# Two-layer decoder trunk on one core: the row sums of layer A's first products move from VectorE to GpSimd and are used one block later

## The chip, the core and the metric

The kernel runs on one core of a Trainium2 chip. The engines are TensorE (PE in the profile, its weight loads PEld), VectorE (DVE), ScalarE (ACT), GpSimd (POOL) and SyncE (SP), which issues the DMA transfers. The metric is the device time of the program in microseconds, as a median over runs; lower is better. A difference is told in microseconds and as a share of the time before.

## The reference, cut to what matters

The program is a two-layer decoder on a sequence of 2048 positions and a width of 1024, in float32. Layer A takes an RMS norm, makes one combined projection into query, key, value, forget logits and gate, attends with a decaying bias, and projects back; layer B shares keys and values and attends in a window of 128. Only the head of layer A is touched by the change:

```python
def rmsnorm(x, g):
    xf = x.astype(jnp.float32)
    y = xf * lax.rsqrt(jnp.mean(xf * xf, axis=-1, keepdims=True) + EPS)
    return (y * g.astype(jnp.float32)).astype(x.dtype)
...
u = rmsnorm(h, norm_a_g[i])
proj = u @ w_in_a[i]
q, k, v, f_logit, gate = jnp.split(
    proj, [WIDTH_A, 2 * WIDTH_A, 3 * WIDTH_A, 3 * WIDTH_A + N_HEADS_A], axis=-1)
```

The gain `g` is folded into the weights, and the factor `rsqrt(mean(x*x) + EPS)` of a row is multiplied in only when the product leaves PSUM.

## The kernel before, in words

The sequence is cut into 16 blocks of 128 positions (`tb`). Layer A's projection runs over seven groups of columns; a group's weights are eight pairs of tiles (`wh` and `wl`, high and low part of 128 rows of the weight matrix, `dt` 0 to 7), and for each block three matmuls per `dt` (high times high, high times low, low times high) add up in one PSUM bank of tag `b2`, of which there are three. Group 0 makes the first half of the values. It is special, since the input arrives during it.

For each block x comes transposed from HBM into a tile `xt` of tag `st` (even blocks, and all from block 12 on) or `wr` (odd blocks). `split_block` makes the high part `uh` on ScalarE (L385) and the low part `ul` on VectorE (L386). Then `block_squares` squares `xt` in place on ScalarE (L391) and adds its eight pieces of 128 columns on VectorE in one TENSOR_REDUCE (L393) into a tile of tag `ro2`, of which there are two. `block_sums` multiplies the two sums of a pair of blocks by a column of ones on TensorE (L402), so that a sum over all 1024 features lies in PSUM; `rstd` (L359 to L365, with one square root on ScalarE, L360) turns it into the factors of both blocks. `v_tile` then takes a block's bank out: a high part on ScalarE (L541) and a low part on VectorE (L542), into a tile of tag `st` (four of them), which one DMA writes to HBM (L545).

`factor(tb, dt)` says when: at an even `tb`, the squares of this block and the next are asked for at `dt` 0, the sums and factors at `dt` 7. `v_tile` of a block follows its last matmul. `constants` makes, among others, `fold` and `identb` from a unit matrix on VectorE (L229 to L234); both are first read in layer A's attention. `vectors`, called at block 8, loads small vectors.

The program text is not the order of execution. A scheduler orders the instructions of each engine when the kernel is built, by what it expects them to cost, within what the tiles allow; each engine then runs its own list strictly in order, and waits on semaphores for others. So what is written later may run earlier, and an instruction that waits holds up all that stand behind it in its engine's list.

Of the kernel before, what the change touches and what calls it, by code (L numbers as in the profile page):

```python
# [18 lines left out]
ALU = mybir.AluOpType  # L19
AX = mybir.AxisListType  # L20
# [3 lines left out]
P = 128  # L24
S = 2048
D = 1024
NTB = S // P
NDT = D // P
# [4 lines left out]
CH = 512  # L33
# [24 lines left out]
NORM_AHEAD = 2  # L58

LOADED_AHEAD = 3  # L60
QK_LAG = 1

FACTOR_AT = 7
ROW_AT = 2

JOBS_AT = (0, 3, 6, 9)
# [85 lines left out]
class Trunk:  # L152
# [56 lines left out]
    def constants(self):  # L209
        nc, cp, a = self.nc, self.const, self.a  # L210

        def select(view, src, pattern, base, cm, fill):
            nc.gpsimd.affine_select(
                out=view, in_=src, pattern=pattern, compare_op=ALU.is_ge,
                fill=fill, base=base, channel_multiplier=cm,
            )

        def tile_(name, shape, dt=F32):
            return cp.tile(shape, dt, name=name, tag=name)

        self.ones = tile_("ones", [P, P])
        nc.gpsimd.memset(self.ones, 1.0)
        self.tri = tile_("tri", [P, P])
        select(self.tri, self.ones, [[1, P]], 0, -1, 0.0)
        self.ident = tile_("ident", [P, P])
        select(self.ident, self.tri, [[-1, P]], 0, 1, 0.0)

        self.fold = tile_("fold", [P, 32])
        nc.vector.tensor_tensor(self.fold, self.ident[:, :32], self.ident[:, 32:64], ALU.add)  # L229
        for c in (64, 96):  # L230
            nc.vector.tensor_tensor(self.fold, self.fold, self.ident[:, c : c + 32], ALU.add)
        nc.vector.tensor_single_scalar(self.fold, self.fold, 2.0, ALU.mult)
        self.identb = tile_("identb", [P, P], BF16)
        nc.vector.tensor_copy(self.identb, self.ident)  # L234

        self.mask_s = tile_("mask_s", [P, 2, P], BF16)
        nc.gpsimd.memset(self.mask_s, 0.0)
        for i in range(2):
            select(self.mask_s[:, i], self.mask_s[:, i], [[1, P]], 0, -1, NEG)

        self.band = tile_("band", [P, 2, P], BF16)
        nc.gpsimd.memset(self.band[:, 0], 0.0)
        select(self.band[:, 0, :], self.band[:, 0, :], [[-1, P]], 0, 1, NEG)
        nc.vector.tensor_tensor(self.band[:, 1], self.tri, self.ident, ALU.subtract)

        self.loads = []
# [24 lines left out]
        self.g_kv = column("g_kv", a["kv_norm_g"], NDT)  # L271
        self.g_qb = pair_column("g_qb", a["qnorm_b_g"][0])
        self.g_kb = pair_column("g_kb", a["knorm_b_g"])
        self.sink = row("sink", a["sinks"], H)
        self.gq16 = row("gq16", a["qnorm_b_g"][:, :ROT], ROT)
# [6 lines left out]

    def vectors(self):

        nc = self.nc
        self.load_vectors(self.loads[1:])
        for t in (self.g_qb, self.g_kb):
            for s in range(2):
                nc.vector.memset(t[s * HD : s * HD + ROT, :], 1.0)

        nc.vector.tensor_single_scalar(self.g_qb, self.g_qb, HD**-0.5, ALU.mult)
# [96 lines left out]
    def block_squares(self, xt):  # L388

        nc = self.nc  # L390
        nc.scalar.activation(xt, xt, AF.Square)  # L391
        sums = self.sb("ro2", [P, P])
        nc.vector.tensor_reduce(sums, xt.rearrange("p (c t) -> p t c", t=P), AX.X, ALU.add)  # L393
        return sums

    def block_sums(self, both, tb):
# [169 lines left out]
    def normer(self, src):  # L566
# [41 lines left out]

        def factor(tb, dt):

            both = (tb, tb + 1)
            if tb % 2:
                return
            if turned and dt == 0:
                for b in both:
                    blocks[b] = self.block_squares(blocks[b])
            if dt == FACTOR_AT:
                sm = self.sb("sm", [P, 4, 8], bufs=4) if turned else small[tb]
                ss = self.block_sums([blocks[b] for b in both], tb) if turned else None
                self.rstd(sm, 2, D, ss=ss, out=factors[:, tb : tb + 2])  # L620

        return upto, factor, uh, ul, factors, fetch

    def projections(self, normed, groups, row, later=None, pre=None, hook=None, first=None):
# [75 lines left out]
        for gi, grp in enumerate(groups):  # L700
# [35 lines left out]
                continue  # L736
            q, v = grp.get("qk"), grp.get("v")
            rope = self.rotary(q["rope"]) if q and "rope" in q else None
            late = []
            for tb in range(NTB):  # L740
                norm(tb + NORM_AHEAD)
                if gi == 1 and tb == ROW_AT:
                    self.rstd_row(factors, row)
                r0 = factors[:, tb : tb + 1]
                if gi == 0 and pre is not None and tb in pre:
                    pre[tb]()
                if tb in FORGET_AT and forget:
                    forget.pop(0)()
                if gi and tb in JOBS_AT and jobs:
                    jobs.pop(0)()  # L750
                us = slice(tb % 4 * P, (tb % 4 + 1) * P)
                ps = self.ps("b2", [P, CH])
                for dt in range(NDT):
                    if hook is not None and gi == len(groups) - 1:
                        hook(tb, dt)
                    if gi == 0:
                        factor(tb, dt)
                    for i, (u, k) in enumerate(((uh, 0), (uh, 1), (ul, 0))):
                        nc.tensor.matmul(  # L759
                            ps[:, :n], u[tb // 4][:, dt, us], W[k][dt],  # L760
                            start=(dt == 0 and i == 0), stop=(dt == NDT - 1 and i == 2),
                        )
                if len(late) > QK_LAG:
                    late.pop(0)()
                if q is not None:
                    c0 = q["c0"]
                    qn = self.qk_norm(
# [9 lines left out]
                if v is not None:  # L777
# [4 lines left out]
                        ),  # L782
                        r0,
                    )
            for job in late:
                job()
            if grp.get("forget"):
# [835 lines left out]
```

## Time and profile before

| What | Value |
|---|---|
| Time, median of 3 runs | 2460.58 us (2459.92 to 2462.29) |
| The profiled execution: its time, its span | 2461.66 us, 2459.7 us |
| PE busy | 2424.1 us, 99% of the span |
| PEld, DVE, ACT, POOL busy | 82%, 70%, 51%, 41% of the span |
| Group 0 of layer A | about 8 to 105 us of the span |

The profile's views that are used: the table of busy times by engine; busy times in stretches of the span; the list of who waited for whom; the timeline of one engine, with the idle time before an instruction and what ended it in brackets; groups of instructions by line and shape with the mean duration of one. The busy share of PE says that the program is bound by TensorE nearly everywhere, so that a change shows in the time only where TensorE waits.

### The profile page before, as it was taken

Reading aid. Unit: us, or ns where it says so; the run is one execution under the profiler, and the core shown is the slowest. Engines: PE = TensorE matmul, PEld = TensorE weight load, DVE = VectorE, ACT = ScalarE, POOL = GpSimd, SP = SyncE. Lnnn points to the kernel's source line nnn. Section 1 sums busy time; section 2 is a strip of 40 time slices with the busy share of each in tenths; the row PEclk is TensorE's granted clock in tenths of the full one; section 3 lists DMA queues with packets and bytes.
Section 4 is the critical chain, followed back from the end, with each engine's and each line's share of the span. In section 5 each row is a group of like instructions: output and inputs, shape, how many; then the busy total and the mean of one; then the engine's idle time right before and its main releaser. Section 6 shows DMA issues by size and latency. Waiting matters only on the chain.

```text
span 2459.7 us, 36240 instructions
## 1 busy us (share of the span) xinstructions
PE 2424.1 (99%) x12016; PEld 2022.4 (82%) x12016; DVE 1727.4 (70%) x3826; ACT 1255.1 (51%) x2504; POOL 1001.9 (41%) x643
## 2 busy tenths in 40 slices
PE   8999999999999999999999999999999999999999
PEld 6788899988888887878877778888788888888887
DVE  7656567735888888888888866456766523777776
ACT  5433324323777777777777761135323312555554
POOL 0000000012877777777778862210011000377775
PEclk9999999999999999999999999999999999999999
DMA  6656545687554655465456649975434415555552
GB/s 181 207 165 193 156 145 168 192 261 223 168 155 128 210 141 150 143 198 164 133 168 182 169 137 306 290 253 153 139 90 120 137 64 165 174 176 178 180 180 73
DMA packets 351515, 419.24 MB, mean 170 GB/s; under 512 B 64928, under 2 KB 248256, under 8 KB 345152
## 3 DMA queue, kind: packets, MB, share of 16 engines
q1 hardware_dynamic: 351328, 416.92, 56.6%
q8 instruction: 95, 1.56, 0.3%
q14 instruction: 92, 0.75, 0.1%
HBM read 265.29 MB, written 151.40 MB: 169 GB/s over the span
## 4 chain that ended last, share of the span: by engine, by line
PE 46%; DVE 4%; DMA 2%; ACT 2%; POOL 2%; issue 2%; SPq 0%; DVEq 0%; ACTq 0%; POOLq 0%
PE b L759 9%; PE b L1240 5%; PE pa L1027 5%; PE pb L1453 4%; PE pb L722 3%; PE pb L1066 3%; PE b L722 3%; PE mx L936 2%; PE sc L985 2%; PE sc L984 2%; PE pa L1383 1%; PE b L1304 1%; PE pa L722 1%; PE pa L1240 1%; PE pb L1240 1%
## 5 line engine op out<-in xcount | busy, mean ns | idle before, releaser
L759 PE MATMUL b<-wh,big 128*128 128x512 f32 (+3 forms) x2560 | 770.1, 375 | 9.8 <-ACT wh L486 8.7
L1003 POOL TENSOR_TENSOR big<-st,big 128x1024 fp32r<-128x1024 f32 (+1 forms) x320 | 657.9, 2070 | 261.4 <-ACT big L1002 155.6
L759 PEld LDWEIGHTS b<-wh,big 128*128 128x128 f32 x2560 | 471.3, 188 | 81.2 <-ACT wh L486 10.5
L759 PE MATMUL b<-wl,big 128*128 128x512 f32 (+3 forms) x1280 | 474.2, 371 | 1.9 <-DVE wl L487 1.9
L1012 DVE TENSOR_TENSOR ac<-ac,st 128x512 f32<-128x512 f32 (+3 forms) x576 | 355.4, 617 | 55.6 <-ACT st L999 27.2
L999 ACT ACTIVATE st<-sc 128x512 f32<-128x512 f32 (+1 forms) x512 | 274.3, 585 | 161.8 <-PE sc L985 79.0
L1027 PE MATMUL pa<-big 128*128 128x512 f32 (+3 forms) x1280 | 326.1, 369 | 3.9 <-POOL big L1003 1.8
L1002 ACT CAST big<-st 128x1024 fp32r<-128x1024 f32 (+1 forms) x320 | 295.6, 924 | 7.8
L759 PEld LDWEIGHTS b<-wl,big 128*128 128x128 f32 x1280 | 241.4, 189 | 38.3 <-DVE wl L487 6.1
L1027 PEld LDWEIGHTS pa<-big 128*128 128x128 f32 x1280 | 222.0, 189 | 50.3 <-ACT sq L1035 17.0
L947 DVE CUSTOM_DVE_ANT_0 mx<-mx,rot 128x128 f32<-128x128 f32 (+3 forms) x240 | 210.7, 878 | 40.9 <-PE mx L936 34.8
L495 ACT ACTIVATE sq<-b,r 128x512 f32<-128x512 f32 (+2 forms) x128 | 77.8, 608 | 301.6 <-PE b L759 298.6
L984 PE MATMUL sc<-big 128*128 128x512 f32 (+3 forms) x640 | 230.1, 364 | 1.3 <-DVE st L542 1.1
L985 PE MATMUL sc<-big 67*128 67x512 f32 (+3 forms) x640 | 229.0, 367 | 0.0
L936 PE MATMUL mx<-big 66*128 66x128 f32 (+3 forms) x660 | 191.1, 363 | 3.6 <-DVE mt L947 3.1
L1066 PE MATMUL pb<-wh,wr 128*128 128x512 f32 x488 | 179.3, 398 | 2.8 <-DMA wr<-wg 2.2
L859 POOL MEMSET rot<- 128x1024 bf16 x1 | 1.0, 952 | 420.8 <-PE pb L349 420.8
L497 DVE TENSOR_REDUCE sm<-sq 128x8 f32<-128x512 f32 (+2 forms) x128 | 74.9, 585 | 138.6 <-ACT sq L495 138.4
L1352 POOL TENSOR_TENSOR big<-big,tri 128x1024 fp32r<-128x1024 f32 x60 | 143.8, 2397 | 67.1 <-DVE big L1349 62.2
L936 PEld LDWEIGHTS mx<-big 66*128 66x128 f32 x660 | 114.1, 190 | 40.9 <-DVE mt L947 11.9
L984 PEld LDWEIGHTS sc<-big 128*128 128x128 f32 x640 | 121.0, 189 | 23.1 <-DVE st L542 1.5
L985 PEld LDWEIGHTS sc<-big 67*128 67x128 f32 x640 | 121.2, 189 | 21.0
(281 smaller groups left out, 4124.8 us busy)
## 6 DMA issues: line engine op xcount, KB each, us to landing
wr<-wg SPq DMA_DIRECT2D x62, 512.0 KB
va<-st SPq DMA_DIRECT2D x32, 512.0 KB
ka<-st SPq DMA_DIRECT2D x64, 256.0 KB
ut<-big SPq DMA_DIRECT2D x16, 1024.0 KB
big<-ka SPq DMA_DIRECT2D x16, 1024.0 KB
big<-qa SPq DMA_DIRECT2D x16, 1024.0 KB
qb<-st SPq DMA_DIRECT2D x64, 256.0 KB
big<-qb SPq DMA_DIRECT2D x16, 1024.0 KB
```

The costliest lines, as they stand in the source:

```text
L722: nc.tensor.matmul(ps, W[k][dt][:, ft * P : (ft + 1) * P], u[ch][:, dt, :], start=(dt == 0 and i == 0), stop=(dt == NDT - 1 and i == 2),)
L759: nc.tensor.matmul(ps[:, :n], u[tb // 4][:, dt, us], W[k][dt], start=(dt == 0 and i == 0), stop=(dt == NDT - 1 and i == 2),)
L936: mm = nc.tensor.matmul(ps[:, b, :wb], qb[:66, i * P : (i + 1) * P], kb[:66, k0 + b * wb : k0 + (b + 1) * wb], start=True, stop=True,)
L947: nc.vector.tensor_tensor_reduce(out=lg, in0=lg, in1=mask, scale=1.0, scalar=NEG, op0=ALU.add, op1=ALU.max, accum_out=f_(o),)
L984: nc.tensor.matmul(o, ka[:, ks], qa[:, qs], start=not (last and n_), stop=False)
L985: nc.tensor.matmul(o, kb[:, ks], qb[:, qs], start=False, stop=not diag)
L999: nc.scalar.activation(pf[:, off : off + w], ps[:, :w], AF.Exp, scale=HD**-0.5)
L1002: nc.scalar.copy(ph[:, :tw], pf[:, :tw])
L1003: nc.gpsimd.tensor_tensor(pl[:, :tw], pf[:, :tw], f_(ph[:, :tw]), ALU.subtract)
L1012: nc.vector.tensor_tensor(a_, a_, pf[:, off : off + w], ALU.add)
L1027: nc.tensor.matmul(pv[:, q0 : q0 + w], v[:, k, :], src[:, off : off + w], start=(p == 0 and n_ == 0 and i == 0), stop=(last and n_ == 1 an ...
L1066: nc.tensor.matmul(ps, w[:, dt // 2 % 2, wk, dt % 2, :], us[dt][uk], start=(dt == 0 and i == 0), stop=(dt == NDT - 1 and i == 2),)
```

## The change

Three things change. (1) The eight pieces of a block's squares are no longer added by one TENSOR_REDUCE on VectorE, but by three adds on GpSimd: 512 columns onto 512, 256 onto 256, and 128 plus 128 into the `ro2` tile. (2) The sums and factors of a pair are asked for at `dt` 3 of the odd block, not at `dt` 7 of the even one; the even block's `v_tile` is held back until then, and both blocks are taken out after it. (3) `fold` and `identb` are made in `vectors` instead of `constants`.

```diff
+TURNED_AT = 3
+
+SQUARES_AT = 6
...
-        nc.vector.tensor_reduce(sums, xt.rearrange("p (c t) -> p t c", t=P), AX.X, ALU.add)
+        for w in (D // 2, D // 4):
+            nc.gpsimd.tensor_tensor(xt[:, :w], xt[:, :w], xt[:, w : 2 * w], ALU.add)
+        nc.gpsimd.tensor_tensor(sums, xt[:, :P], xt[:, P : 2 * P], ALU.add)
         return sums
...
-            both = (tb, tb + 1)
-            if tb % 2:
-                return
-            if turned and dt == 0:
-                for b in both:
+            t0 = tb // 2 * 2
+            if turned and (tb, dt) == (t0, 0 if tb else SQUARES_AT):
+                for b in (t0, t0 + 1):
                     blocks[b] = self.block_squares(blocks[b])
-            if dt == FACTOR_AT:
+            if (tb, dt) == ((t0 + 1, TURNED_AT) if turned else (t0, FACTOR_AT)):
...
+                        if held and dt == TURNED_AT:
+                            held.pop()()
...
+                if gi == 0 and pre is not None and tb % 2 == 0:
+                    held.append(partial(evict, ps, tb))
+                else:
+                    evict(ps, tb)
```

What this makes of the engines' lists is seen at three places. On VectorE, at the start of the program, in rows that split the first weights (`wl`) and add the first squares (`ro2`), before:

```order
L487 SCALAR_TENSOR_TENSOR wl_139<-big_122,g_a_111,wh_138 128x512
L487 SCALAR_TENSOR_TENSOR wl_143<-big_122,g_a_111,wh_142 128x512
L393 TENSOR_REDUCE ro2_176<-st_123 128x128
L229 TENSOR_TENSOR fold_88<-ident_86 128x32
L234 CAST identb_93<-ident_86 128x128
L231 TENSOR_TENSOR fold_88<-fold_88,ident_86 128x32
L244 TENSOR_TENSOR band_103<-tri_84,ident_86 128x128
L231 TENSOR_TENSOR fold_88<-fold_88,ident_86 128x32
L487 SCALAR_TENSOR_TENSOR wl_147<-big_122,g_a_111,wh_146 128x512
```

and now:

```order
L494 SCALAR_TENSOR_TENSOR wl_134<-big_117,g_a_106,wh_133 128x512
L494 SCALAR_TENSOR_TENSOR wl_138<-big_117,g_a_106,wh_137 128x512
L243 TENSOR_TENSOR band_98<-tri_84,ident_86 128x128
L287 TENSOR_TENSOR fold_88<-ident_86 128x32
L291 CAST identb_89<-ident_86 128x128
L289 TENSOR_TENSOR fold_88<-fold_88,ident_86 128x32
L494 SCALAR_TENSOR_TENSOR wl_142<-big_117,g_a_106,wh_141 128x512
```

The reduce is gone from between the second and the third `wl`; the small constants stand there still, although the program text now has them at block 8.

On GpSimd, in the first microseconds, before:

```order
L242 MEMSET band_103 128x128
L213 AFFINE_SELECT band_103<-band_103 128x128
L859 MEMSET rot_5206 128x1024
L860 AFFINE_SELECT rot_5206<-rot_5206 128x128
```

and now (`st_118`, `wr_125` and `st_127` are the x of blocks 0, 1 and 2):

```order
L241 MEMSET band_98 128x128
L399 TENSOR_TENSOR st_118<-st_118 128x512
L217 AFFINE_SELECT band_98<-band_98 128x128
L399 TENSOR_TENSOR st_118<-st_118 128x256
L400 TENSOR_TENSOR ro2_189<-st_118 128x128
L399 TENSOR_TENSOR wr_125<-wr_125 128x512
L399 TENSOR_TENSOR wr_125<-wr_125 128x256
L400 TENSOR_TENSOR ro2_194<-wr_125 128x128
L399 TENSOR_TENSOR st_127<-st_127 128x512
```

GpSimd had nothing to do in group 0 behind the masks; now 48 adds stand there, three for each of 16 blocks.

On ScalarE, near the end of group 0, where block 15's x (`st_711`, now `st_735`) is split and squared and blocks 12 and 13 are taken out (`st_756` and `st_787`, now `st_796` and `st_815`); `sm` is the square root for a pair's factors, `cossin` the sine for layer B's rotary tables. Before:

```order
L385 CAST big_653<-st_711 128x8x128
L360 ACTIVATE sm_743<-sm_743 128x2
L391 ACTIVATE st_711<-st_711 128x1024
L329 ACT_TABLE_LOAD
L329 ACTIVATE cossin_676<-cossin_676 128x256
L541 ACTIVATE st_756<-b2_715,r_121 128x8x64
L541 ACTIVATE st_787<-b2_762,r_121 128x8x64
```

and now:

```order
L334 ACT_TABLE_LOAD
L334 ACTIVATE cossin_686<-cossin_686 128x256
L390 CAST big_663<-st_735 128x8x128
L396 ACTIVATE st_735<-st_735 128x1024
L365 ACT_TABLE_LOAD
L365 ACTIVATE sm_786<-sm_786 128x2
L548 ACTIVATE st_796<-b2_739,r_116 128x8x64
L548 ACTIVATE st_815<-b2_776,r_116 128x8x64
```

The square root of blocks 12 and 13, and with it their way out of PSUM, now stands behind block 15's split, its squares and a second table load. Past group 0 and the first two blocks of group 1 every engine's list is as before.

## Rows read from the trace of the kernel before

**Rows 1.** The page: span, then busy time, share and instructions of each engine.

```profile
span 2459.7 us, 36240 instructions
PE 2424.1 (99%) x12016; PEld 2022.4 (82%) x12016; DVE 1727.4 (70%) x3826; ACT 1255.1 (51%) x2504; POOL 1001.9 (41%) x643
```

**Rows 2.** A stretch: length, busy PE, PEld, DVE, ACT, POOL, granted clock, DMA, GB/s.

```profile
75.00:100.00 25.00, 24.06 (x110) 19.62 (x109) 19.42 (x41) 13.81 (x17) 0.00 (x0) 1.00 0.56 154
```

**Rows 3.** Who PE waited for in 0 to 130 us: total, times, longest.

```profile
PE b L759 <- ACT wh L486: 8.2, 1, 8.2
PE b L759 <- DVE wl L487: 1.4, 2, 1.2
PE pa L402 <- DVE ro L393: 1.2, 3, 0.6
```

**Rows 4.** Timeline of PE: start, duration, instruction, idle before and its releaser.

```profile
10.89 1.05 PE L759 MATMUL b<-wh,big 128*128 128x512 f32 x2
13.10 0.50 PE L759 MATMUL b<-wl,big 128*128 128x512 f32 x1 [1.16 <-DVE wl L487]
13.44 0.61 PE L759 MATMUL b<-wh,big 128*128 128x512 f32 x2
...
20.80 0.38 PE L402 MATMUL pa<-ones,ro 128*128 128x1 f32 x2 [0.25 <-DVE ro L393]
...
62.57 0.50 PE L402 MATMUL pa<-ones,ro 128*128 128x1 f32 x4
...
73.95 0.50 PE L402 MATMUL pa<-ones,ro 128*128 128x1 f32 x4
...
85.96 0.38 PE L402 MATMUL pa<-ones,ro 128*128 128x1 f32 x2 [0.34 <-DVE ro L393]
98.08 0.38 PE L402 MATMUL pa<-ones,ro 128*128 128x1 f32 x2 [0.60 <-DVE ro L393]
```

**Rows 5.** Timeline of DVE and ACT at the start.

```profile
9.77 1.98 DVE L393 TENSOR_REDUCE ro<-st 128x128 f32<-128x1024 f32 x1
12.30 0.74 DVE L487 SCALAR_TENSOR_TENSOR wl<-big,g_a,wh 128x512 fp32r<-128x512 f32 x1
...
8.70 1.04 ACT L391 ACTIVATE st<-st 128x1024 f32<-128x1024 f32 x1
```

**Rows 6.** Groups by shape on POOL: busy, mean ns of one, idle before.

```profile
L1194 POOL TENSOR_TENSOR wh<-wh,wl 128x512 f32<-128x512 f32 x29 | 37.6, 1296 | 127.5 <-DMA wl<-oc 102.3 <-DVE big L1200 18.1 <-DVE big L138 4.8
L1364 POOL TENSOR_TENSOR wl<-wl 128x256 f32<-128x256 f32 x15 | 11.1, 737 | 1.0
```

**Rows 7.** Timeline of POOL and DVE in layer A's output projection.

```profile
1476.74 1.30 POOL L1194 TENSOR_TENSOR wh<-wh,wl 128x512 f32<-128x512 f32 x1 [3.52 <-DMA wl<-oc]
...
1476.20 0.69 DVE L1198 TENSOR_TENSOR qn<-qn 128x512 f32<-128x512 f32 x1
1476.80 1.79 DVE L1198 TENSOR_TENSOR wh<-wh 128x512 f32<-128x512 f32 x1
```

**Rows 8.** Groups by shape in 0 to 100 us: busy, mean ns, idle before.

```profile
L386 DVE TENSOR_TENSOR big<-st,big 128x1024 fp32r<-128x1024 f32 x10 | 12.2, 1223 | 12.5 <-ACT big L385 12.5
L385 ACT CAST big<-st 128x1024 fp32r<-128x1024 f32 x10 | 10.5, 1050 | 12.5 <-DMA st<-in_x_t 12.5
L542 DVE SCALAR_TENSOR_TENSOR st<-b,r,st 128x512 fp32r<-128x512 f32 x14 | 10.1, 746 | 5.1 <-ACT st L541 5.0
```

**Rows 9.** Timelines of SP and ACT around the loads of blocks 14 and 15.

```profile
81.61 0.34 SPq L371 DMA_DIRECT2D st<-in_x_t  x1
87.05 1.53 SPq L371 DMA_DIRECT2D st<-in_x_t  x1
...
85.11 1.05 ACT L385 CAST big<-st 128x1024 fp32r<-128x1024 f32 x1
92.64 1.05 ACT L385 CAST big<-st 128x1024 fp32r<-128x1024 f32 x1 [2.36 <-DMA st<-in_x_t]
98.95 1.28 ACT L360 ACT_TABLE_LOAD   x1
```

More of the change, by code (lines that the diff above doesn't have):

```diff
@@ L228, in constants @@
         self.fold = tile_("fold", [P, 32])
[L229 to L232, printed above, removed]
         self.identb = tile_("identb", [P, P], BF16)
-        nc.vector.tensor_copy(self.identb, self.ident)
         self.mask_s = tile_("mask_s", [P, 2, P], BF16)
@@ L286, in vectors @@
         self.load_vectors(self.loads[1:])
+        nc.vector.tensor_tensor(self.fold, self.ident[:, :32], self.ident[:, 32:64], ALU.add)
+        for c in (64, 96):
+            nc.vector.tensor_tensor(self.fold, self.fold, self.ident[:, c : c + 32], ALU.add)
+        nc.vector.tensor_single_scalar(self.fold, self.fold, 2.0, ALU.mult)
+        nc.vector.tensor_copy(self.identb, self.ident)
         for t in (self.g_qb, self.g_kb):
@@ L609, in factor @@
         def factor(tb, dt):
-            both = (tb, tb + 1)
-            if tb % 2:
-                return
-            if turned and dt == 0:
-                for b in both:
+            t0 = tb // 2 * 2
+            if turned and (tb, dt) == (t0, 0 if tb else SQUARES_AT):
+                for b in (t0, t0 + 1):
                     blocks[b] = self.block_squares(blocks[b])
-            if dt == FACTOR_AT:
+            if (tb, dt) == ((t0 + 1, TURNED_AT) if turned else (t0, FACTOR_AT)):
                 sm = self.sb("sm", [P, 4, 8], bufs=4) if turned else small[tb]
-                ss = self.block_sums([blocks[b] for b in both], tb) if turned else None
-                self.rstd(sm, 2, D, ss=ss, out=factors[:, tb : tb + 2])
+                ss = self.block_sums([blocks[b] for b in (t0, t0 + 1)], tb) if turned else None
+                self.rstd(sm, 2, D, ss=ss, out=factors[:, t0 : t0 + 2])
         return upto, factor, uh, ul, factors, fetch
@@ L738, in projections, with evict @@
             rope = self.rotary(q["rope"]) if q and "rope" in q else None
[L739 to L743, printed above, removed]
-                r0 = factors[:, tb : tb + 1]
[L745 to L764, printed above, removed]
+            late, held = [], []
+            def evict(ps, tb):
+                nonlocal z
+                r0 = factors[:, tb : tb + 1]
                 if q is not None:
@@ L784, in projections @@
                     )
+            for tb in range(NTB):
+                norm(tb + NORM_AHEAD)
+                if gi == 1 and tb == ROW_AT:
+                    self.rstd_row(factors, row)
+                if gi == 0 and pre is not None and tb in pre:
+                    pre[tb]()
+                if tb in FORGET_AT and forget:
+                    forget.pop(0)()
+                if gi and tb in JOBS_AT and jobs:
+                    jobs.pop(0)()
+                us = slice(tb % 4 * P, (tb % 4 + 1) * P)
+                ps = self.ps("b2", [P, CH])
+                for dt in range(NDT):
+                    if hook is not None and gi == len(groups) - 1:
+                        hook(tb, dt)
+                    if gi == 0:
+                        factor(tb, dt)
+                        if held and dt == TURNED_AT:
+                            held.pop()()
+                    for i, (u, k) in enumerate(((uh, 0), (uh, 1), (ul, 0))):
+                        nc.tensor.matmul(
+                            ps[:, :n], u[tb // 4][:, dt, us], W[k][dt],
+                            start=(dt == 0 and i == 0), stop=(dt == NDT - 1 and i == 2),
+                        )
+                if len(late) > QK_LAG:
+                    late.pop(0)()
+                if gi == 0 and pre is not None and tb % 2 == 0:
+                    held.append(partial(evict, ps, tb))
+                else:
+                    evict(ps, tb)
             for job in late:
```

## The prediction, on record before the changed kernel ran

> **What bounds the kernel now.** I read the table of engines first. TensorE (PE) is busy 2424.1 of 2459.7 us [rows 1], so the time can only move where PE waits: 35.6 us in all, 8.2 of them before its first matmul. Next I read stretches of group 0 of layer A, which the change touches: from 75 to 100 us PE is short of 25 us by 0.94, VectorE is busy for 19 and GpSimd not at all [rows 2]. The list of waits then says what PE waited for up to 130 us: 8.2 us for the first weights, which no edit touches, 1.4 us for `wl`, and 1.2 us, in three waits, for the row sums that VectorE makes [rows 3]. The timeline gives the places: 1.16 us at 13.10, 0.25 at 20.80, 0.34 at 85.96 and 0.60 at 98.08 [rows 4]; what is left of the 1.4 us for `wl`, some 0.2, is one more short wait. This is 2.6 us, 0.11% of the time: the most that the change can give back, unless it makes PE wait elsewhere, and then the loss has no such bound.
>
> **The change part by part.** Durations are from the profiled execution, so the sum stands against its 2461.66 us. Its span lies 1.96 us below that, and it is 1.08 us over the median of 2460.58; I add the same sum to the median.
>
> *Start of the program.* VectorE's reduce of block 0 (1.98 us) stood from 9.77, and five small constants behind it, so that the third `wl` began at 12.30 [rows 5], and PE waited for it [rows 4]. The reduce goes; the constants stay in front of the third `wl`, in spite of the program text. If GpSimd did not touch VectorE, this `wl` would begin as soon as its `wh` is there. ScalarE makes that behind block 0's squares, which end at 9.74 (8.70 + 1.04) [rows 5], in about the 0.7 us of a `wl`: at 10.4, and the wait of 1.16 us would be gone. But at 9.74 GpSimd's first add begins. Its 512-column add takes 1.30 us in this kernel [rows 6], and beside one such add, begun at 1476.74, a VectorE add with two operands in SBUF took 1.79 us where the one before it took 0.69 [rows 7]: it stood still until GpSimd was through, 1476.74 + 1.30 = 1478.04, and then ran. The constants and the `wl` are of that kind. So they wait until about 9.8 + 1.3 = 11.1; with 0.3 for the constants the `wl` begins at 11.4, 0.9 us sooner than before. If GpSimd's second add (0.74) also goes first, it is 0.2 sooner. I take -0.6, from -1.2 (no standing still) to 0. One more bound belongs here: two matmuls begun at 10.89 took 1.05 us, two of the same form begun at 13.44 took 0.61 [rows 4], though the profile prints a granted clock of 1.00 [rows 2]. So one costs 0.2 us more at the first level (1.2 GHz) than at the second (2.4 GHz). Should a PE that no longer pauses stay at the low one until 13.1, three matmuls pay that, and 0.6 us of the gain is lost; this is inside the bounds.
>
> The Trainium skill ("SBUF — State Buffer", section "Who interferes with whom") says that VectorE and GpSimd share a port pair as an exclusive lock, that a VectorE instruction with two SBUF inputs contends with a GpSimd instruction that reads SBUF, and that `tensor_reduce` on trn2 never does. Rows 7 agree with the first half. By this rule the change swaps a sum that disturbs nobody for 48 that stop the splits; by it the total is my forecast, without it the first rival.
>
> *Sums of block 1.* PE's sums of blocks 0 and 1 now come in the middle of block 1's matmuls. Block 1's squares need its split on VectorE (1.22), which follows the last `wl`: six of some 0.7 each from 11.4, so 15.5, then the split to 16.8 and ScalarE's squares (1.04) to 17.9. GpSimd's three adds are 1.30 + 0.74 + 0.45 = 2.5 us (256 columns fewer save 0.56, so 128 fewer 0.28: 0.74 - 0.28 = 0.46) [rows 6]. They meet two more splits of 1.22 us [rows 8], of blocks 2 and 3, in turns: done between 20.4 and 22.8. PE gets there at about 19.5 (block 1 begins some 16.2, then 14 matmuls of 0.23). So it waits 0.9 to 3.3 us; without standing still 0.3. Before it waited 0.25. I take 1.75, net +1.5, bounds 0 to +2.8.
>
> *Later sums.* The waits of 0.34 and 0.60 us go, since PE asks four `dt` into the odd block, 12 matmuls after the old place: -0.94. I keep 0 as the other bound for a late block 15.
>
> *Later evictions.* This is the new wait. PSUM has three banks for these products, so block b+3 needs block b's bank. Before, sums at the end of the even block left some 12 us until that; now there are about 9, in lists where the eviction stands behind splits that wait for x. For block 13 and block 10's bank: x of block 14 is loaded into the tile of block 12, which is free when GpSimd's 128-column add has run, and this add needs a `ro2` tile that PE frees with its sums, nine matmuls and the sums, 2.05 + 0.25 us, into block 11. Then 0.45 add, 0.35 issue, 3.5 to 4.1 until landing (81.61 to 85.11; 88.58, the end of the issue, to 92.64) [rows 9], 1.05 cast, 1.22 split, 0.75 eviction, and an estimated 0.45 for a step of the sine and for handing over: 10.1 to 10.7 after block 11's start, and 1.3 more when a split stands still. Two blocks with their sums are 11.38 us (73.95 - 62.57, so a matmul 0.227) [rows 4]. So PE waits 0 to 0.6.
>
> For block 15 and block 12's bank: from block 10's eviction on, two issues of 0.35, landing 3.5 to 4.1, cast 1.05, split 1.22, squares 1.04, a table load of 1.28 [rows 9], an estimated 0.95 for the square root and four small steps, eviction 0.75 on each engine [rows 8]: 11.3 to 11.9, up to 13.2 with one turn lost, since the square root now stands behind block 15's squares. Against 11.38 that is 0 to 1.8 us. The same chain at blocks 7, 9 and 11 has 2 to 3 us to spare without turns; with three lost turns (3.9) it is late by up to 1 each. I take 0.3 + 1.1 + 0.6 = +2.0 for all, bounds 0 to +5.
>
> *The next group.* Its first weights follow the same releases, with VectorE less loaded: the 0.2 left over in [rows 3] goes, if it lies there. Everything behind is unchanged and bound by PE, so it shifts whole. Making the constants costs the same at its old place; VectorE's 32 us of reduces were hidden under PE in all but the waits named.
>
> Sum: -0.6 + 1.5 - 0.9 + 2.0 - 0.2 = **+1.8 us**: 2463.5 for an execution like the profiled one, 2462.4 beside the median.
>
> **Rivals.**
> 1. *No turns, waits simply go.* GpSimd's adds run in gaps of VectorE, which is busy only 19 of 25 us [rows 2]. Then -1.2 at the start, 0 at block 1, -0.9, +0.2 at block 15, -0.2: -2.1 us, 2458.5. Against it speak rows 7.
> 2. *Slower, by late evictions.* One mechanism: a turn lost in a pair's split makes its eviction late, the eviction makes the next x load late (SP issues it behind the eviction's store), and so the next pair. It decides as soon as three lost turns (3.9 us) exceed the 2 to 3 us to spare at blocks 7 to 11, so that PE waits 1 to 1.5 us at four or five blocks: -0.3 + 2 - 0.9 + 5.5 = +6.3 us, 2466.9. For it: the list puts the splits of later blocks ahead of a pair's factors, and the small factor steps also have two operands in SBUF. Against it: each turn needs both engines at the same moment, and GpSimd has 40 us of work in 100.
> 3. *The change does not do what it says.* The constants do not move, as the lists show; that part alone is worth 0. If the scheduler's other moves cancelled the rest, the time stays within 0.5 us: 2460.6.
>
> **How the numbers follow.** Chances: forecast 0.45, rival 1 0.30, rival 2 0.17, rival 3 0.08. Two tenths of a per cent, 4.9 us, is about what this measurement can tell from no change. Only rival 2 passes it, and not always, but the upper bound of the forecast's evictions does too: slower 0.16. To be faster by as much is beyond the 2.6 us of waits there are: 0.02. The rest, 0.82, is no change. Range 2457.8 to 2467.0: rival 1 with 0.6 us for the spread of the runs below, rival 2 above. The forecast's own range is 2460 to 2465.5.
>
> **What would show it.** The first: PE's wait at 13.10 shrunk and moved to 11 or 12 us; VectorE rows of `wl` or splits in group 0 of 1.5 us or more beside GpSimd adds. The second: a PE wait of 1 to 3 us for GpSimd's `ro` near 20 us. The third: no sum waits at 86 and 98, but PE waits for VectorE's `st` at the first matmul of blocks 13 and 15. Wrong would be: `wl` and splits at 0.75 and 1.22 throughout with no PE wait after 25 us (rival 1), waits at blocks 7, 9 and 11 of a microsecond each (rival 2), or a time that moved outside group 0.

## The result, and the profile after

The changed kernel takes 2466.29 us (median of 18 runs, 2462.76 to 2470.07), the kernel before in the same comparison 2461.64 (18 runs, 2458.31 to 2463.72): a ratio of 1.0021, with a 95% interval of 1.0015 to 1.0028. That is 4.65 us slower by the medians (0.19%) and 0.21% by the ratio. It lies inside the range given, but 2.9 us above the forecast of +1.8. The prediction took two tenths of a per cent, 4.9 us, for the limit of what can be told from no change; the interval, some 1.6 us to either side, excludes no change, so that limit was too wide.

The profiled execution of the changed kernel took 2464.55 us. Its page answers to [rows 1]: GpSimd has 44 us more to do, VectorE 20 less, and TensorE (PE) is as busy as before in a span that is 3.1 us longer.

```profile
span 2462.8 us, 36308 instructions
PE 2423.5 (98%) x12016; PEld 2021.6 (82%) x12016; DVE 1707.8 (69%) x3810; ACT 1254.5 (51%) x2504; POOL 1045.7 (42%) x691
```

Who PE waited for in the first 130 us, as in [rows 3] (in all, times, longest): 14.1 us, where it was 10.8.

```profile
PE b L790 <- ACT wh L493: 9.6, 2, 8.6
PE pa L409 <- POOL ro L400: 1.6, 1, 1.6
PE b L790 <- DVE st L549: 1.3, 1, 1.3
PE b L790 <- DVE g_qb L294: 1.3, 1, 1.3
PE b L790 <- DVE wl L494: 0.3, 1, 0.3
```

The timeline of PE gives the places, as in [rows 4]. The pause for the third `wl` is gone (the matmul at 12.44 bears no wait). New are 1.62 us for GpSimd's sums of block 1, and two waits for the bank of an evicted block: 1.28 us before block 9 (the row names `g_qb`, a constant that VectorE makes beside block 6's eviction) and 1.34 us before block 15. The next group waits 0.94 us for a `wh`. The last row is the transpose of the row factors in the third block of group 1: all that group 0 did to the time has happened there. Before, this transpose began at 116.71; now it is 4.85 us later.

```profile
8.62 0.80 PE L790 MATMUL b<-wh,big 128*128 128x512 f32 x1 [8.62 <-ACT wh L493]
...
12.44 0.79 PE L790 MATMUL b<-wl,big 128*128 128x512 f32 x1
...
16.52 0.61 PE L790 MATMUL b<-wh,big 128*128 128x512 f32 x2
...
22.54 0.38 PE L409 MATMUL pa<-ones,ro 128*128 128x1 f32 x2 [1.62 <-POOL ro L400]
...
66.44 0.47 PE L790 MATMUL b<-wh,big 128*128 128x512 f32 x1 [1.28 <-DVE g_qb L294]
...
102.50 0.47 PE L790 MATMUL b<-wh,big 128*128 128x512 f32 x1 [1.34 <-DVE st L549]
...
114.03 0.49 PE L790 MATMUL b<-wh,big 128*128 128x512 f32 x1 [0.94 <-ACT wh L493]
...
121.56 0.27 PE L354 MATMUL pa<-ident,r 128*16 128x128 f32 x1
```

VectorE and GpSimd at the start, as in [rows 5] and [rows 7]: VectorE's 32-column add takes 1.27 us beside GpSimd's 512-column add (another such add, at 15.47 in the kernel with six banks, took 0.18), and the third `wl` begins at 11.56 instead of 12.30. GpSimd pays as well: its 256-column add takes 1.17 us where [rows 6] have 0.74.

```profile
10.21 1.39 POOL L399 TENSOR_TENSOR st<-st 128x512 f32<-128x512 f32 x1 [7.73 <-ACT st L396]
10.37 1.27 DVE L289 TENSOR_TENSOR fold<-fold,ident 128x32 f32<-128x32 f32 x1
11.56 4.81 DVE L494 SCALAR_TENSOR_TENSOR wl<-big,g_a,wh 128x512 fp32r<-128x512 f32 x6
11.80 1.17 POOL L399 TENSOR_TENSOR st<-st 128x256 f32<-128x256 f32 x1
```

The last x load and what follows it, as in [rows 9]. SP issues x of block 15 right behind the store of block 10's eviction; both are 2.3 us later than before (89.30 against 87.05), ScalarE's cast of block 15 is 2.0 us later (94.59 against 92.64), and the eviction of blocks 12 and 13 (`st<-b,r`) stands behind that cast, the squares, a table load and the square root. PE itself was 2.7 us later by then (block 9 began at 66.44, before at about 63.7 by the count of matmuls), so beside PE this load is not late; what the rows show is the order in which the eviction stands.

```profile
88.06 0.74 DVE L549 SCALAR_TENSOR_TENSOR st<-b,r,st 128x512 fp32r<-128x512 f32 x1
88.83 0.37 SPq L552 DMA_DIRECT2D va<-st  x1
89.30 0.52 SPq L376 DMA_DIRECT2D st<-in_x_t  x1
94.59 1.05 ACT L390 CAST big<-st 128x1024 fp32r<-128x1024 f32 x1 [0.92 <-DMA st<-in_x_t]
97.00 1.06 ACT L396 ACTIVATE st<-st 128x1024 f32<-128x1024 f32 x1 [1.35 <-DVE sm L364]
98.07 1.28 ACT L365 ACT_TABLE_LOAD   x1
...
100.88 1.26 ACT L548 ACTIVATE st<-b,r 128x512 fp32r<-128x512 f32 x2 [1.31 <-issue]
101.61 1.41 DVE L549 SCALAR_TENSOR_TENSOR st<-b,r,st 128x512 fp32r<-128x512 f32 x2 [0.81 <-ACT st L548]
```

### The profile page after: what moved, and what is told of

It is laid out like the page before. It is cut to its first block, busy times and chain, and to the rows that moved or that the text cites. A ratio compares the mean times of both kernels' runs of the same rounds, so it can differ in the third digit from the quotient of the medians.

```text
span 2462.8 us, 36308 instructions
## 1 busy us (share of the span) xinstructions
PE 2423.5 (98%) x12016; PEld 2021.6 (82%) x12016; DVE 1707.8 (69%) x3810; ACT 1254.5 (51%) x2504; POOL 1045.7 (42%) x691
## 4 chain that ended last, share of the span: by engine, by line
PE 46%; DVE 4%; ACT 2%; DMA 2%; POOL 2%; issue 2%; DVEq 0%; ACTq 0%; POOLq 0%; SPq 0%
PE b L790 10%; PE b L1255 5%; PE pa L1042 4%; PE pb L1468 4%; PE pb L727 3%; PE pb L1081 3%; PE b L727 3%; PE mx L951 2%; PE sc L1000 2%; PE sc L999 2%; PE pa L1398 1%; PE b L1319 1%; PE pa L1255 1%; PE pb L1255 1%; PE pa L727 1%
## 5 line engine op out<-in xcount | busy, mean ns | idle before, releaser
L790 PEld LDWEIGHTS b<-wh,big 128*128 128x128 f32 x2560 | 471.9, 189 | 85.0 <-ACT wh L493 11.4
L517 POOL TENSOR_TENSOR ro<-qn,rot 128x64 f32<-128x64 f32 (+1 forms) x48 | 15.7, 327 | 297.3 <-DVE qn L508 297.3
```

What stands on the lines that cost most here:

```text
L790: nc.tensor.matmul(ps[:, :n], u[tb // 4][:, dt, us], W[k][dt], start=(dt == 0 and i == 0), stop=(dt == NDT - 1 and i == 2),)
```

## The experiments

The change has three parts: GpSimd adds the squares (engine), sums and evictions come later (postponement), and constants are made later. With the postponement goes a small change that the diff shows (`SQUARES_AT`): the first pair's squares are asked for at `dt` 6 of block 0, not at `dt` 0. The theory that I began with was the prediction's: turns between GpSimd and VectorE, and a longer chain, make it slow. The rival was that the postponement is enough, whatever engine adds. Ratios are to the kernel before in the same comparison; "transpose" is the start of the row factors' transpose in the profiled execution (116.71 before). What lies behind that point differed from the kernel before by -3.5 to +3.7 us in these single executions, so the ratio judges a kernel, and the transpose only tells what group 0 did.

| kernel | median us | ratio, 95% interval | transpose |
|---|---|---|---|
| changed kernel | 2466.29 | 1.0021 (1.0015 to 1.0028) | 121.56 |
| engine alone | 2460.12 | 0.9997 (0.9988 to 1.0006) | 115.90 |
| constants alone | 2461.07 | 1.0001 (0.9992 to 1.0009) | 117.54 |
| engine and constants | 2459.76 | 1.0002 (0.9994 to 1.0011) | 118.50 |
| postponed, VectorE adds | 2466.45 | 1.0021 (1.0012 to 1.0030) | 120.10 |
| evictions held, sums not | 2464.81 | 1.0017 (1.0008 to 1.0027) | 121.05 |
| first pair alone postponed | 2465.86 | 1.0021 (1.0012 to 1.0030) | 123.48 |
| sums at dt 0, not dt 3 | 2466.68 | 1.0032 (1.0020 to 1.0044) | 123.94 |
| six banks, not three | 2469.36 | 1.0038 (1.0025 to 1.0052) | 125.17 |
| split behind eviction | 2463.02 | 1.0017 (1.0008 to 1.0026) | 121.01 |
| the same, first pair as before | 2464.49 | 1.0021 (1.0012 to 1.0030) | 120.66 |
| sine later | 2466.04 | 1.0025 (1.0016 to 1.0034) | 122.38 |
| split behind, sine later | 2465.68 | 1.0018 (1.0009 to 1.0027) | 120.99 |

**The engine alone.** The kernel before, with:

```diff
-        nc.vector.tensor_reduce(sums, xt.rearrange("p (c t) -> p t c", t=P), AX.X, ALU.add)
+        for w in (D // 2, D // 4):
+            nc.gpsimd.tensor_tensor(xt[:, :w], xt[:, :w], xt[:, w : 2 * w], ALU.add)
+        nc.gpsimd.tensor_tensor(sums, xt[:, :P], xt[:, P : 2 * P], ALU.add)
```

> The kernel before, with one edit: the row sums of the squares are GpSimd's three halving adds in place of VectorE's reduce. The sums stay at the end of the even block, evictions are not held, constants stay at the start. Theory (GpSimd's adds and VectorE's two-operand instructions stop each other, and the adds are a longer chain than the reduce): the third wl begins earlier (-0.6), but PE's sums now wait for GpSimd: 1.5 to 2 us in block 0 or 1, and 0.5 to 1.5 us in two or three later pairs; in all +2 to +4 us, 2464 to 2466. Rival 1 (the postponement, not the engine, makes the change slow): 0 to -1 us, since VectorE is freed at the start, and sums wait no longer than the 1.2 us of before.

Measured: 0.9997 (0.9988 to 1.0006), no loss. PE's waits up to 130 us in this kernel, less than in [rows 3]:

```profile
PE b L761 <- ACT wh L488: 8.1, 2, 7.8
PE b L761 <- DVE wl L489: 0.8, 1, 0.8
PE pa L404 <- POOL ro L395: 0.2, 1, 0.2
```

The turns are all there. In the same kernel's timeline of GpSimd and VectorE an add of 128 columns takes 1.38 us and a split 1.48, beside GpSimd's adds. PE's wait for the third `wl`, which stands behind that add, is 0.77 us all the same, where it was 1.16, and for a sum it waits 0.18.

```profile
9.42 1.28 POOL L394 TENSOR_TENSOR st<-st 128x512 f32<-128x512 f32 x1 [6.95 <-ACT st L391]
9.48 1.38 DVE L244 TENSOR_TENSOR band<-tri,ident 128x128 bf16<-128x128 f32 x1
...
19.11 1.48 DVE L386 TENSOR_TENSOR big<-wr,big 128x1024 fp32r<-128x1024 f32 x1 [0.93 <-ACT big L385]
```

My theory fell here: the cost of 2 to 4 us that it expected of the engine is excluded by the interval, which ends at +1.5 us.

**The postponement alone.** The changed kernel, with the reduce on VectorE in place of the adds (the diff above the other way round).

> The changed kernel, with one edit: the sums of squares are VectorE's reduce again. Sums stay in the middle of the odd block, evictions held, constants late. No GpSimd adds, so no turns. Theory: the sums are never waited for (-1.2 us), the wait for the third wl is shorter by the constants (-0.3 to -0.6), evictions have 9 us instead of 12 with VectorE 19 us busy of 25, so 0 to 1 us of bank waits: -2 to 0 us beside the kernel before, 2459.5 to 2461.5. Rival 1 (postponement makes it slow, by late evictions, whatever engine adds): +2.5 to +5 us as the changed kernel, 2464 to 2466.5, with bank waits of over a microsecond each at two or more blocks.

Measured: 1.0021 (1.0012 to 1.0030), the ratio of the whole change. GpSimd adds nothing in group 0 here, so there are no turns; the third `wl` and the next group's `wl` cost 1.0 us, the next group's `wh` 0.9, and PE waits twice for a bank, before block 3 and before block 13. These are the timeline's two rows:

```profile
31.29 0.47 PE L788 MATMUL b<-wh,big 128*128 128x512 f32 x1 [1.29 <-DVE st L547]
...
89.97 0.47 PE L788 MATMUL b<-wh,big 128*128 128x512 f32 x1 [1.50 <-DVE st L547]
```

The wait at block 3 can be followed on VectorE: the first step of the factor of blocks 0 and 1 runs at 22.20, the last at 28.59, and between them stand two splits and two reduces of later blocks, 6.5 us in all. So an eviction can be late by the order of the list alone.

The rival stands: the postponement makes the loss, with either engine.

**The constants alone, and both other parts together.** The five lines of `fold` and `identb` moved to `vectors()` as in the change, once with the reduce and once with GpSimd's adds.

> The kernel before, with one edit: the five small constants are made with the vectors, as in the changed kernel. Theory: the third wl follows the reduce and one other constant, some 0.4 us sooner, so PE's wait of 1.16 us at 13.1 is 0.6 to 0.8: -0.4 us, 2461.2, no difference that is measured. Rival (a PE that pauses less early on only runs longer at its slow pace): 0. Should it be +1 or more, the constants at their new place are in the way of the splits.

> The kernel before, with two of the three parts of the change: GpSimd's adds, and the constants made with the vectors. Sums stay at the end of the even block, nothing is held. If the postponement alone is what costs time, this is the change without its loss: 0 to -2 us beside before, 2459 to 2461, with no wait for banks, and PE's wait for the third wl, 0.77 with GpSimd's adds alone, 0.3 or less. How much of that reaches the end is open, since PE was at its slow pace until 16.3 us there. If GpSimd's turns with VectorE were to cost, it would be 2462 to 2464.

Measured: 1.0001 (0.9992 to 1.0009) and 1.0002 (0.9994 to 1.0011). With the reduce the wait for the third `wl` shrank from 1.16 to 0.72 us, as expected. With GpSimd's adds it is gone, but PE then waits 1.84 us for block 1's sums at 22.27 and falls back to its slow pace for 3 us (rows at the end); in the time nothing is won. What the change does apart from the postponement is worth between -1.5 and +2.7 us by the interval.

**Six banks.** In the changed kernel, group 0:

```diff
-                ps = self.ps("b2", [P, CH])
+                if gi == 0 and pre is not None:
+                    if tb % 2 == 0:
+                        pair = self.ps("b2", [P, 2, CH])
+                    ps = pair[:, tb % 2]
+                else:
+                    ps = self.ps("b2", [P, CH])
```

> The changed kernel, with one edit: in group 0 the products of an even and an odd block share one tile of two PSUM banks, so that six banks stand for blocks, not three, and block 6 is the first that waits for an eviction (of blocks 0 and 1). Theory (late evictions cost 2.6 us of the change): both waits at the first matmul of blocks 9 and 15 (1.28 and 1.34 us with handing over) go; left are 1.6 us for the sums of block 1 and the waits of the next group: 2463 to 2464 (-2.5 beside the changed kernel). Rival 2 (the next x loads or the next group's weights are late behind the evictions' stores anyway): PE waits for a split or for wh of the next group instead, 2465.5 to 2466.5.

Measured: 1.0038 (1.0025 to 1.0052), slower still. PE waits 2.77 us at 40.47, the first matmul of block 4, and the trace names an eviction (by its time, 39.66 + 0.75, that of block 2), which with six banks block 4 should not need. Why it waits there I can't say; the edit did not take the waits away as meant, and on the banks this run decides nothing. It shows one thing: block 1's eviction, at 34.00, stands on ScalarE behind the cast of a block whose x comes at 33.05, after ScalarE has waited 3.64 us for it.

From this came two theories of the postponement: A, the evictions have too few microseconds; B, they stand behind splits in the lists, since the held eviction follows the split of block b+2 in the program.

**Time, order and the sine.** Three edits of the changed kernel: A `TURNED_AT = 0`; B the split behind the eviction; then `ANGLES_AT = 15`, which takes the sine and its table load out of block 15's way. Edit B:

```diff
-                norm(tb + NORM_AHEAD)
+                if not (held and tb % 2):
+                    norm(tb + NORM_AHEAD)
...
                             held.pop()()
+                            norm(tb + NORM_AHEAD)
```

> The changed kernel, with one number changed: TURNED_AT is 0, so a pair's sums and the even block's eviction come at the first dt of the odd block, 9 matmuls or 2.05 us sooner; the lists of ScalarE and VectorE keep nearly the same order. Theory A (since the sums come later, evictions have too little time, and what matters is the microseconds): the waits of 1.28 and 1.34 us for banks go to 0, and those of the next group (0.94 and 0.29) to 0.25; the wait for block 1's sums stays 1.6 to 2.5: 2462 to 2464, against 2466.3 of the changed kernel. Theory B (what matters is that the held eviction stands in the lists behind splits that wait for x): the gain is under 1 us, 2465 to 2466.5.

> The changed kernel, with one edit: in odd blocks of group 0 the split of block b+2 is issued behind the held eviction, not ahead of it. The sums stay at the fourth dt of the odd block. In the lists of ScalarE and VectorE a pair's evictions now stand ahead of the cast and split of the odd block b+2, which wait for x. Theory B (the list order is the cause): no wait for banks at blocks 9 and 15; -2.6, and up to -1 at the next group; left is the wait for block 1's sums: 2462.5 to 2464. Theory A (too little time): both bank waits stay, 2465.5 to 2467.

> The changed kernel, with one number changed: ANGLES_AT is 15, so the sine and its table load come behind the evictions of blocks 12 and 13 in the lists. Theory: block 12's eviction is sooner by the table load (1.28 us) and some of VectorE's steps of the sine; the bank wait of 1.34 us at block 15 goes; that of 1.28 at block 9 and the 1.6 for block 1's sums stay: -1.3, 2464 to 2465.5. Rival (the eviction waits for block 15's x anyway, whose load is late): the wait stays over 1 us, 2465.5 to 2467.

> Both edits in the changed kernel: the split of block b+2 behind the held eviction, and the sine at block 15. Theory: no wait for banks in group 0 at all; left are 1.6 us for block 1's sums and 1 to 1.6 at the next group's weights: 2461 to 2463, 0 to +2 beside before. If a bank wait of over 0.5 us is left at any block, 9 us from the sums are too few whatever the lists say.

Measured: none of the four gets back to the kernel before, and their intervals overlap that of the change, so neither edit alone undoes the loss. B's time lies in the range that theory B gave for it (2463.02), but the kernel before was faster in that comparison (2459.61), and by the ratio no gain can be told; the waits were not those of the theory. Each edit removes at least one wait it was aimed at, and others come up. With A block 9 no longer waits, but blocks 13 and 15 do, 1.87 and 0.91 us. With B block 9 no longer waits, but block 13 does, 1.73 us, since on VectorE the steps of the sine now stand ahead of the eviction of block 10, whose bank it needs. A turn is part of it: the two steps shown first take 0.37 and 0.29 us in the changed kernel, and here run beside GpSimd's adds of 86.58 to 88.68. Block 15 still waits 0.51.

```profile
86.76 1.21 DVE L331 TENSOR_SCALAR cossin<-cossin 128x128 f32<-128x128 f32 x1
88.00 0.83 DVE L332 TENSOR_TENSOR cossin<-cossin 128x128 f32<-128x128 f32 x1
88.75 0.74 DVE L549 SCALAR_TENSOR_TENSOR st<-b,r,st 128x512 fp32r<-128x512 f32 x1
```

With the sine later block 15's wait went, block 9's fell to 0.78, and one of 1.90 us came at 112.31, in group 1, whose bank waits for an eviction at 111.4. With both edits PE still waits 0.68 us at 109.74 for an eviction and 1.11 at 111.78 for a `wh`.

**The first pair.** Once as in the kernel before, beside edit B (squares, sums and eviction of blocks 0 and 1 not postponed); once the other way round: engine and constants, with the first pair alone postponed, to dt 6 of block 1.

> As the kernel with the split behind the held eviction, and the first pair (blocks 0 and 1) as in the kernel before: its sums at the end of block 0, its eviction not held. Theory B: the wait of 1.6 us for block 1's sums shrinks to 0.2, as with GpSimd's adds alone, and no bank waits: 2460 to 2462. Theory A: 2464 to 2466.

> GpSimd's adds and the constants made with the vectors, as in the run of these two parts, but now the first pair alone is postponed: the sums of blocks 0 and 1 stand at the seventh dt of block 1, and block 0's eviction is held to there; all later pairs have their sums at the end of the even block and nothing held. Theory: PE gets to block 1's sum 2 us after GpSimd's last add, so the wait of 1.84 us at 22.3 goes, and block 3, 5.5 us later, finds block 0's bank free: -1.5 beside that run, 2457.5 to 2459, faster than before by 1 to 2 us. Rival: 5.5 us aren't enough for factor and eviction behind the splits of later blocks in the lists; block 3 then waits 1 to 2 us, and the time is that run's, 2459.5 to 2461.

Measured: 1.0021 (1.0012 to 1.0030) and again 1.0021 (1.0012 to 1.0030). In the first, GpSimd's sum of block 1 is waited for all the same (1.88 us at 22.14), and 0.43 and 0.24 us for banks. The second was meant to beat both kernels, and costs as much as the whole change: x of block 6 is late (0.74 and 0.53 us at 47.69 and 48.95), and at 103.08 PE waits 2.76 us for the sum of block 15. Its x is loaded at 90.77, behind an eviction's store and the sine's load of the positions, 6.4 us later than in engine and constants (84.38). Its split begins at 97.98, as soon as its cast has ended (96.75 + 1.06), so the late load holds the sum, and not the sine's steps on VectorE.

**The evictions alone.** Engine and constants as above (sums at the end of the even block), with the change's holding of the even block's eviction to dt 3 of the odd block:

```diff
+                        if held and dt == TURNED_AT:
+                            held.pop()()
...
+                if gi == 0 and pre is not None and tb % 2 == 0:
+                    held.append(partial(evict, ps, tb))
+                else:
+                    evict(ps, tb)
```

> As the run of GpSimd's adds and late constants (sums at the end of the even block), with one part of the postponement alone: the even block's eviction is held to the fourth dt of the odd block, so it stands behind the split of block b+2 in the program. Theory B (late evictions behind splits are what the postponement costs): PE waits for banks 1 us or more at two or more blocks, +2 to +4 beside that run: 2462 to 2464.5. If the later place of the sums is what costs, and not that of the eviction: 2459 to 2461 and no bank waits.

Measured: 1.0017 (1.0008 to 1.0027): holding the eviction is enough for the loss. The waits are not where I expected them: for a bank only 0.33 us, but 1.89 for the sums of blocks 14 and 15 at 102.28 (the 1.89 for block 1's sums at 22.02 has its like, 1.84, in the kernel without holding). Both kernels' timelines of VectorE, SP and ScalarE show why; the last row of each is PE at the sums of blocks 12 and 13. Not held, block 10's eviction runs at 82.50, its store is issued at 83.28, and x of block 15 behind it at 84.38:

```profile
82.50 0.75 DVE L544 SCALAR_TENSOR_TENSOR st<-b,r,st 128x512 fp32r<-128x512 f32 x1 [0.81 <-ACT st L543]
83.28 0.37 SPq L547 DMA_DIRECT2D va<-st  x1
84.38 1.70 SPq L371 DMA_DIRECT2D st<-in_x_t  x1
89.63 1.05 ACT L385 CAST big<-st 128x1024 fp32r<-128x1024 f32 x1 [3.27 <-DMA st<-in_x_t]
88.44 0.50 PE L404 MATMUL pa<-ones,ro 128*128 128x1 f32 x4
```

Held, the same four steps come 5.8 to 6.5 us later, while PE is 0.3 sooner:

```profile
88.99 0.73 DVE L549 SCALAR_TENSOR_TENSOR st<-b,r,st 128x512 fp32r<-128x512 f32 x1
89.76 0.37 SPq L552 DMA_DIRECT2D va<-st  x1
90.22 0.53 SPq L376 DMA_DIRECT2D st<-in_x_t  x1
96.01 1.05 ACT L390 CAST big<-st 128x1024 fp32r<-128x1024 f32 x1 [1.34 <-DMA st<-in_x_t]
88.14 0.50 PE L409 MATMUL pa<-ones,ro 128*128 128x1 f32 x4
```

So here the eviction is a link of the loop that feeds x: SP's list is in order, the store waits for the eviction, and the load of x of block 15 stands behind the store. The load of x of block 13, behind block 8's store, is 6.2 us later in the same way (76.51 against 70.31). It is not so throughout: x of blocks 8, 10, 11 and 12 is loaded 1.6 to 3.7 us sooner than in the kernel without holding, since the lists differ. Nor does every loss rest on this link. In the kernel that is postponed with VectorE's adds x of block 15 is loaded at the following time, sooner than the 87.05 of [rows 9], and it loses as much, by late evictions that make PE wait for banks:

```profile
85.26 0.34 SPq L376 DMA_DIRECT2D st<-in_x_t  x1
```

Of the twelve kernels and the changed one, the three that hold no eviction lose nothing (0.9997 to 1.0002), and the ten that hold at least one lose 1.0017 to 1.0038.

## Why the prediction was right or wrong

*Start of the program, -0.6.* The turns came as described: constants until 11.56, where 11.4 was worked out, and the wait of 1.16 us gone. Nearly all was lost to the slow pace: the 14th matmul from the third `wl` on began 7.90 us after the first matmul (16.52 - 8.62), before 8.06 (16.29 - 8.23). That is -0.16, near the end of the bounds for which the text gave this reason. The first matmul itself was 0.39 later, which no edit explains.

*Sums of block 1, +1.5.* Right in kind and size: 1.62 us waited, 1.75 foreseen; beside the 0.25 of before +1.37.

*Later sums, -0.94.* Right: no wait for sums after 23 us.

*Later evictions, +2.0.* 1.28 + 1.34 = +2.62 us. Block 15 was foreseen with 1.1 and waited 1.34; block 13 waited 0, not 0.3; block 9, one of three with 0.6 together, 1.28. The reason given beside it, lost turns, is seen at block 9: on the way to block 6's eviction a split and two steps of the factor stand still beside GpSimd's adds and take 1.66 us more than alone (1.22, 0.16 and 0.16), which is more than the wait:

```profile
59.89 1.55 DVE L391 TENSOR_TENSOR big<-st,big 128x1024 fp32r<-128x1024 f32 x1 [3.29 <-ACT big L390]
62.86 1.06 DVE L367 TENSOR_TENSOR sm<-sm 128x2 f32<-128x2 f32 x1
64.15 0.59 DVE L370 SCALAR_TENSOR_TENSOR r<-sm 128x2 f32<-128x2 f32 x1
```

At block 15 turns are 0.45 of the 1.34 us (the same two steps at 99.80 and 100.48). The loss as a whole does not need them: without GpSimd's adds the waits are 1.29 and 1.50, at blocks 3 and 13.

*The next group, -0.2.* This step failed, in sign: 0.94 + 0.29 us were waited, 0.25 before, +0.98. The text said that these weights "follow the same releases, with VectorE less loaded". They follow block 15, and what is late there is late here, and some more: their next two loads are issued at 105.01 one behind the other, and ScalarE's last casts come at 113.26, behind a wait for DMA; before, the loads went out at 101.92 and 103.90. The last two pairs of casts come 3.5 and 4.0 us later than before, and PE began block 15 3.3 us later (102.50 against about 99.2 by the count of matmuls). These are the changed kernel's rows:

```profile
105.01 2.16 SPq L447 DMA_DIRECT2D wr<-in_w_in_a  x2
110.09 1.34 ACT L493 ACTIVATE wh<-wr,g_a 128x512 fp32r<-128x512 f32 x2 [0.58 <-DMA wr<-in_w_in_a]
113.26 1.33 ACT L493 ACTIVATE wh<-wr,g_a 128x512 fp32r<-128x512 f32 x2 [1.83 <-DMA wr<-in_w_in_a]
```

The terms as measured are -0.16 + 1.37 - 0.94 + 2.62 + 0.98 = +3.87, with the later first matmul +4.26; the transpose is 4.85 later. The 0.59 between are not assigned: matmuls behind a wait also run some slower (0.31 us from 102.50 to the next one, against 0.23). So the places are those foreseen, but for the next group, and the terms were mis-sized: the next group by 1.2 and the evictions by 0.6, and a start that gave 0.4 less.

That the waits of one trace add up to the loss is no proof that each is a cause. Engine and constants waits 1.84 us for block 1's sums and loses nothing in the time (1.0002); postponed with VectorE's adds never waits for them and loses as much as the whole change. What the experiments show to cost is the held eviction, the +2.0 of the sum, with either engine.

*The range.* The time lay inside it because it reached to the second rival. The forecast's own range, 2460 to 2465.5, ends below the 2466.29 measured; the kernel before was 1.06 us slower in this comparison than the 2460.58 of the prediction, and with that taken off the time is 2465.2, just inside. This is the width of the range and not its precision.

*The rivals.* The first, no turns, is refuted by the rows, but its conclusion on the engine is what was measured: with turns and all, GpSimd's adds alone cost nothing. The Trainium skill's rule ("SBUF — State Buffer", section "Who interferes with whom") agrees with this trace, 1.27 us for an add of 32 columns; that each such stop would be paid for at the end, as I concluded from it, is what the engine alone excludes. The second rival, +6.3 by a late eviction that makes the next x load late, is the link that shows where evictions alone are held, and its size is nearer to the +4.65 measured than the forecast's. In the changed kernel itself neither half of it is borne out: three lost turns stand before one wait, with 1.66 us and not 3.9, and the load of block 15 is no later than PE is. What starts it in the experiments is holding: engine and constants has the turns and no late load, and with the first pair alone postponed, one eviction held, the load of block 15 is 6.4 us later. The third, that the constants do nothing, is right in the time (1.0001), though the wait for the third `wl` shrank from 1.16 to 0.72 us.

What stays open: which wait takes the loss in a given kernel, and which share the late bank and the late x load have in it. It moved with each edit of the order, I have one profiled execution of each, and in eight of the experiments a stretch of lower granted clock is mixed in (last section). A kernel faster than before was not found; engine alone, at 0.9997, cannot be told from it.

## What to carry to other kernels

When an eviction is put off, look at what its steps stand behind in the engines' lists, and at what its store stands ahead of in the queue that issues loads: with the evictions alone held, two of the later input loads came some 6 us later while PE was at the same place, and the loss came up five blocks behind the eviction. Here each of four edits took a wait out, and other waits came up; undo the parts of a change one by one before mending the waits of the new trace. An engine swap that stops another engine for 1.3 us a time cost nothing here, where that engine has 6 us in 25 to spare; on a path that was tight already, as to the bank of block 9, the same stops are seen in a wait.

## What the runs showed of the hardware

VectorE's smallest instructions with two operands in SBUF can pay nearly a whole turn: the 128x2 multiply of the factor took 1.06 us at 62.86 and 81.46 in the changed kernel, beside a GpSimd add of 512 columns, and 0.16 at 75.58, with none beside it, and in the kernel before.

A wait of PE can cost more than its length. In the kernel with engine and constants the matmuls behind the wait at 22.27 follow each other in 0.23 us, and from 24 us on in 0.43; the granted clock of that stretch is 0.50, the first level (1.2 GHz). About seven matmuls at 0.2 us more are 1.4 us, which no list of waits shows. In the changed kernel nothing of the kind followed the waits of 1.62 and 1.34. Stretches of 0.50 or little above stand before 120 us in seven more experiments, all but engine alone, constants alone, postponed with VectorE's adds and split behind eviction; the kernel before and the changed kernel have none, so the clock is not what the change loses by in group 0. Where PE waited 1.62 to 1.64 us for block 1's sums, the clock fell in two kernels (six banks; split behind, sine later) and not in three (changed; split behind; sine later). PE's timeline, then the stretch (columns as in [rows 2]):

```profile
22.27 0.38 PE L404 MATMUL pa<-ones,ro 128*128 128x1 f32 x2 [1.84 <-POOL ro L395]
...
24.02 0.63 PE L761 MATMUL b<-wl,big 128*128 128x512 f32 x1
24.45 1.05 PE L761 MATMUL b<-wh,big 128*128 128x512 f32 x2
```

```profile
24.00:27.00 3.00, 3.00 (x8) 2.31 (x7) 1.05 (x2) 1.24 (x2) 2.77 (x5) 0.50 0.77 298
```

At the start of the program the profile prints a granted clock of 1.00 all the same, while matmuls follow each other in 0.43 us, the spacing of the stretch at 0.50 above (1.00 in 9 to 13 us of the kernel before; the stretch in [rows 2], which the prediction named for this, is 75 to 100 us). When they change to 0.23 differs by more than the waits that the change was to remove: by 14.9 us in the changed kernel, where PE did not pause; by 16.6, 16.6 and 17.9 in the three with a pause of 0.72 to 0.77 us (engine alone, postponement alone, constants alone); and by 13.4 in the kernel before, behind its pause of 1.16. Each is one execution.
